# NSA compressed branch and SSD diagonal products issued in another form in a two-layer decoder trunk (one Trainium2 core)

## Chip, cores and metric

The kernel runs on one core of one Trainium2 chip. The metric is the device time of one execution in microseconds (us), lower is better. Before the change it is 2308.91 us, the median of 3 runs (2308.01 to 2309.33).

## The reference

A causal sequence of 256 tokens with 2048 channels goes through two layers, all in float32. Layer 0 mixes with Mamba-2 SSD (16 heads of 64 channels) beside MoBA attention (8 heads of 128); layer 1 mixes with NSA attention (8 query heads, 2 key/value heads of 128) beside retention (8 heads). Each layer ends in a convolutional feed-forward part, and every half layer in a layer norm. What matters here is two sums.

NSA adds three gated attentions for every query head; with 256 tokens the selected blocks and the window both hold all past keys, and the compressed branch has 15 keys per key/value head:

```
k_cmp = compress(kc, ...); v_cmp = compress(vc, ...)     # 15 rows of 128 per kv head
logits_c = q . k_cmp * scale + bias_c;  p_cmp = masked_softmax(logits_c, cmp_mask);  o_cmp = p_cmp . v_cmp
o = g[..., 0:1] * o_cmp + g[..., 1:2] * o_sel + g[..., 2:3] * o_win
```

SSD's part inside its one chunk of 256 tokens is, per head:

```
y_diag = einsum('bgcls,bghcls,bcsghp->bclghp', cb, decay, xdt_g)
```

## The kernel before

Weights stream from HBM in slabs of up to 128 x 1024 values: SP issues the DMA to `wraw` (L102), ScalarE rounds it to the float32r part `whi` (L108), VectorE takes the rest as `wlo` (L109). TensorE multiplies both with activations that lie in SBUF as such pairs. `group_b` (L277) holds weights as the stationary operand; for each 128 rows of the contraction it issues two products of 512 columns with `whi` and two of 256 columns with `wlo` (L314). Here these are called the plain products.

The small work of the mixers is cut into steps and put in a queue, `Fill`. `fill.pop()` after every second contraction step of a group of one output takes the next step out; a step can be empty. So the order of TensorE is: plain products, one step, plain products, one step. The framework then orders the instructions of each engine with a cost model of its own, and each engine works through its queue in order; it puts the semaphore waits in.

`attn_steps` (L599) makes three steps for a head: `scores`, `normalise`, `mix`. It serves MoBA's heads (one branch, no compressed keys) and NSA's (two branches, `ks` and `kw`, with `cmp`). `pair` (L595) queues two heads in turn: two empty steps, scores of both, an empty step, normalise of both, an empty step, mix of both. In `scores` each branch makes the products of 128 queries by 128 keys and 128 by 256 in one PSUM tile `S` (L611, L612); NSA's first branch adds two products with 7 and 15 compressed keys (L615, L616). `softmax` adds bias and finds the row limit on VectorE (L589) and takes exponentials on ScalarE (L592). `normalise` scales by the sum's reciprocal times the gate (L635, for the compressed part L649), turns three tiles of 128 x 128 per branch (L639) and the two compressed ones (L652, L653) and copies them out of PSUM (L642, L644, L655, L656). `mix` (L673) sums, for the first 128 queries and then the other 128, values times turned probabilities: one product per branch in the first half, two in the second, and in each half one with 7 or 15 rows of compressed values `vcmp`. A float32 product is recorded as two loads of the stationary operand and two passes.

`compress` (L1002) makes the compressed keys and values; its step `project` ends with one product for the keys (L1034) and two of 15 columns for the values (L1038), copied into `vcmp`. In `ssd_steps` (L761), `decay` makes the 128 x 384 factor `L` of a head and `diag(ct)` multiplies two heads: three products of 64 columns each (L846 to L848), head 0 into the lower 64 partitions of a PSUM tile and head 1 into the upper 64, all three of head 0 before those of head 1. `odd` (L897) lays out layer 1's buffers; GpSimd only raises to powers there (L199 in the norm ahead of it, L1086 in retention).

Of the kernel before, what the change touches and what calls it, by code (L numbers as in the profile page):

```python
# [9 lines left out]
F32 = mybir.dt.float32  # L10
F32R = mybir.dt.float32r
AF = mybir.ActivationFunctionType
# [248 lines left out]
class Trunk:  # L261
# [321 lines left out]

    def softmax(self, P, S, nb0, nb1, w0, w1, z, stat, j):

        nc = self.nc
        mn = P.tile([128, 2], F32, name="mn", bufs=4)
        for i, (c, n, nb) in enumerate(((0, w0, nb0), (w0, w1, nb1))):
            nc.vector.tensor_tensor_reduce(out=z[:, c:c + n], in0=S[:, c:c + n], in1=nb, scale=SCALE, scalar=3e38,  # L589
                                           op0=OP.add, op1=OP.min, accum_out=mn[:, i:i + 1])  # L590
        for i, (c, n) in enumerate(((0, w0), (w0, w1))):
            nc.scalar.activation(z[:, c:c + n], z[:, c:c + n], AF.Exp, scale=-1.0, bias=mn[:, i:i + 1],  # L592
                                 accum_out=stat[:, j + i:j + i + 1])

# [4 lines left out]
    def attn_steps(self, P, y, ct, h, branches, gate=None, cmp=None):  # L599

        nc = self.nc
        st = {}
        nbr = len(branches)
        ncol = 2 * nbr + (2 if cmp else 0)

        def scores():
            stat = P.tile([128, 8], F32, name="stat", bufs=4)
            st["stat"], st["z"] = stat, []
            for b, (q, k, _) in enumerate(branches):
                S = self.ps()  # L610
                nc.tensor.matmul(S[:, 0:128], q[:, 0:128], k[:, 0:128], start=True, stop=True)  # L611
                nc.tensor.matmul(S[:, 128:384], q[:, 128:256], k, start=True, stop=True)  # L612
                if b == 0 and cmp:
                    kc = cmp[0]
                    nc.tensor.matmul(S[:, 384:391], q[:, 0:128], kc[:, 0:7], start=True, stop=True)  # L615
                    nc.tensor.matmul(S[:, 391:406], q[:, 128:256], kc, start=True, stop=True)  # L616
                z = P.tile([128, 384], F32, name="z", bufs=self.zbufs)
                self.softmax(P, S, self.nb[:, h, 128:256], self.nb[:, h, :], 128, 256, z, stat, 2 * b)
                st["z"].append(z)
                if b == 0 and cmp:  # L620
                    zc = P.tile([128, 22], F32, name="zc", bufs=4)
                    self.softmax(P, S[:, 384:406], self.nb[:, h, 159:256:16], self.nb[:, h, 31:256:16], 7, 15, zc,
                                 stat, 2 * nbr)
                    st["zc"] = zc

        def normalise():
            stat = st["stat"]
            nc.vector.reciprocal(stat[:, :ncol], stat[:, :ncol])
            if gate is not None:
                nc.vector.tensor_tensor(stat[:, :ncol], stat[:, :ncol], gate, op=OP.mult)  # L630
            st["pt"] = []
            for b in range(nbr):
# [12 lines left out]
                st["pt"].append(ptS)  # L645
            if cmp:
                zc = st["zc"]
                for i, (c, n) in enumerate(((0, 7), (7, 15))):
                    nc.vector.tensor_scalar(zc[:, c:c + n], zc[:, c:c + n],  # L649
                                            stat[:, 2 * nbr + i:2 * nbr + i + 1], None, op0=OP.mult)  # L650
# [6 lines left out]
                st["ptc"] = ptc  # L657

        def mix():
            o = self.ps()  # L660
            for t in range(2):
                mms = []
                for b, (_, _, v) in enumerate(branches):
                    pt = st["pt"][b]
                    if t == 0:
                        mms.append((v(0), pt[:, 0:128]))
                    else:
                        mms += [(v(0), pt[:, 128:256]), (v(1), pt[:, 256:384])]
                if cmp:
                    n = 7 if t == 0 else 15  # L670
                    mms.append((cmp[1][:n, :], st["ptc"][:n, t * 128:(t + 1) * 128]))
                for i, (a, b) in enumerate(mms):
                    nc.tensor.matmul(o[:, t * 128:(t + 1) * 128], a, b, start=(i == 0), stop=(i == len(mms) - 1))  # L673
            self.split(y[:, ct, :256], y[:, ct, 256:], o[:, :256])

        return scores, normalise, mix


# [82 lines left out]
    def ssd_steps(self, P, y, dt, xs, bc, zs, mask):  # L761
# [135 lines left out]
    def odd(self):  # L897
        nc, x = self.nc, self.x
        with ExitStack() as ctx:
            self.zbufs = 4  # L900
            with self.tc.tile_pool(name="odd2", bufs=1) as P2:
# [5 lines left out]
                gates = P2.tile([128, H, 6], F32, name="gates")  # L907
                kv = {n: P2.tile([128, 2, 256], F32, name=n) for n in ("ks", "kw")}
                kcmp = P2.tile([128, 30], F32, name="kcmp")
                vcmp = P2.tile([15, 2, 128], F32, name="vcmp")  # L910
                row = P2.tile([128, 1], F32, name="row")
# [45 lines left out]
                for i in range(2):  # L957
                    self.group_b(self.xk, [ev_cmp(i)])
                for i, n in enumerate(("ks", "kw")):
                    self.group_b(self.xk, [lambda acc: self.sum_halves(P2, kv[n], acc)])  # L960
                    self.compress(P2, i, *xbs[i], kcmp, vcmp)
                self.load_bias(P2, P2)
# [3 lines left out]
                for i in range(4):  # L966
# [3 lines left out]
                    for j in range(2):  # L970
# [4 lines left out]
                            P2, y, h, h,  # L975
                            [(q[:, j, :], kv["ks"][:, e, :], lambda t, sl=sl: vs[:, t, sl]),
                             (q[:, j, :], kv["kw"][:, e, :], lambda t, sl=sl: vw[:, t, sl])],
                            gate=gates[:, h, :], cmp=(kcmp[:, 15 * e:15 * e + 15], vcmp[:, e, :])))
                    self.pair(heads)
# [21 lines left out]

    def compress(self, P, i, xh, xl, kcmp, vcmp):  # L1002

# [4 lines left out]
        for s in range(4):  # L1008
# [6 lines left out]
            if s == 3:  # L1015
                rows = P.tile([34, 256], F32, name="crow", bufs=1)
                nc.scalar.activation(rows, acc, AF.Copy)
# [13 lines left out]
        def project():  # L1031
            u, o = st["u"], self.ps()
            if i == 0:
                nc.tensor.matmul(o[:, :30], self.w2[:, 0, :], u, start=True, stop=True)  # L1034
                nc.vector.tensor_copy(kcmp, o[:, :30])
            else:
                for e in range(2):
                    nc.tensor.matmul(o[:15, e * 128:(e + 1) * 128], u[:, 15 * e:15 * e + 15], self.w2[:, 1, :],  # L1038
                                     start=True, stop=True)
                nc.vector.tensor_copy(vcmp.rearrange("p a b -> p (a b)"), o[:15, :256])  # L1040

# [225 lines left out]
```

## Time and profile before

| | before |
|---|---|
| median of 3 runs | 2308.91 us (2308.01 to 2309.33) |
| profiled execution | 2309.18 us, its span 2307.4 us |
| mean granted TensorE clock | 0.998 |
| TensorE busy | 2293.4 us, 99% of the span |
| VectorE, ScalarE, GpSimd busy | 61%, 48%, 1% |
| HBM traffic | 188 GB/s over the span |

The span runs from the first to the last instruction. TensorE's matmuls are pipelined, so the recorded length of one is longer than the time that it holds the engine; the distance between the starts of instructions is what is read. NSA's steps lie between 1304 and 1400 us, SSD's diagonal products between 163 and 221 us.

### The profile page before, as it was taken

The numbers are of one execution on the slowest core, as the hardware profiler recorded it, in microseconds if no ns is written. First come the engines' busy times: TensorE is split into PE (matmuls) and PEld (weight loads), VectorE is DVE, ScalarE is ACT, GpSimd is POOL, SyncE is SP. The second block draws the span as 40 slices with busy tenths as digits, with TensorE's granted clock in tenths as the row PEclk, the third lists the DMA queues.
The fourth block names the chain that finished last, engine by engine and source line by source line (L and its number), as shares of the span: only waits on it lengthen the run. The fifth ranks groups of instructions, "written<-read, shape, count | busy, mean of one in ns | idle before, by whom it ended". The sixth has DMA issues, their size and how long they took to land.

```text
span 2307.4 us, 32010 instructions
## 1 busy us (share of the span) xinstructions
PE 2293.4 (99%) x12550; PEld 1981.4 (86%) x12550; DVE 1418.0 (61%) x1921; ACT 1105.0 (48%) x1429; POOL 21.6 (1%) x32
## 2 busy tenths in 40 slices
PE   9999999999999999999999999999999999999998
PEld 9888888888888888888889888889888888888886
DVE  5687667666666665445645667767666666654445
ACT  5555543555555554334345554444545555543332
POOL 0001000000000000000000000000000000000000
PEclk9999999999999999999999999999999999999999
DMA  8664464666666666667557634584666666676664
GB/s 279 199 188 149 162 226 153 202 191 185 190 189 189 189 197 217 193 193 221 176 166 217 212 108 141 167 269 129 192 189 189 190 190 185 190 226 194 193 194 142
DMA packets 128249, 436.63 MB, mean 189 GB/s; under 512 B 14257, under 2 KB 16993, under 8 KB 127713
## 3 DMA queue, kind: packets, MB, share of 16 engines
q1 hardware_dynamic: 128096, 434.58, 60.9%
q8 instruction: 98, 1.61, 0.3%
q14 instruction: 55, 0.44, 0.1%
HBM read 432.41 MB, written 2.11 MB: 188 GB/s over the span
## 4 chain that ended last, share of the span: by engine, by line
PE 98%; DMA 1%; DVE 1%; ACT 0%; issue 0%; SPq 0%; POOL 0%; DVEq 0%; ACTq 0%; POOLq 0%
PE acc L314 57%; PE acc L353 10%; PE acc L355 10%; PE acc L354 10%; PE ps L353 1%; PE ps L354 1%; PE ps L355 1%; PE ps L673 1%; DMA wraw<-in_ev_in 1%; PE acc L338 1%; PE ps L314 0%; PE ps L252 0%; PE ps L612 0%; PE ps L639 0%; PE ps L338 0%; PE acc L345 0%
## 5 line engine op out<-in xcount | busy, mean ns | idle before, releaser
L109 DVE TENSOR_TENSOR wlo<-wraw,whi 128x1024 fp32r<-128x1024 f32 (+4 forms) x794 | 949.2, 1198 | 635.4 <-ACT whi L108 634.2
L314 PE MATMUL acc<-x,whi 128*128 128x512 f32 x3776 | 1178.3, 397 | 0.0
L108 ACT ACTIVATE whi<-wraw 128x1024 fp32r<-128x1024 f32 (+4 forms) x794 | 822.6, 1037 | 728.6 <-PE acc L355 285.8
L314 PEld LDWEIGHTS acc<-x,wlo 128*128 128x128 f32 x3776 | 692.4, 188 | 156.6 <-issue 0.2
L314 PE MATMUL acc<-x,wlo 128*128 128x256 f32 x3776 | 726.1, 279 | 0.0
L314 PEld LDWEIGHTS acc<-x,whi 128*128 128x128 f32 x3776 | 584.3, 189 | 12.5 <-issue 1.2
L353 PE MATMUL acc<-whi,A 128*128 128x512 f32 x448 | 175.9, 393 | 0.0
L405 ACT ACTIVATE tmp<-acc 128x512 f32<-128x512 f32 x120 | 71.8, 598 | 215.5 <-PE acc L314 215.5
L355 PE MATMUL acc<-whi,A 128*128 128x512 f32 x448 | 174.6, 390 | 0.0
L354 PE MATMUL acc<-wlo,A 128*128 128x512 f32 x448 | 174.5, 390 | 0.0
L353 PE MATMUL acc<-whi,B 128*128 128x512 f32 x388 | 150.9, 389 | 0.0
L354 PE MATMUL acc<-wlo,B 128*128 128x512 f32 x388 | 150.9, 389 | 0.0
L355 PE MATMUL acc<-whi,B 128*128 128x512 f32 x388 | 150.9, 389 | 0.0
L355 PEld LDWEIGHTS acc<-whi,A 128*128 128x128 f32 x448 | 84.1, 188 | 17.7 <-DVE A L274 0.3
L353 PEld LDWEIGHTS acc<-whi,A 128*128 128x128 f32 x448 | 84.1, 188 | 17.3 <-ACT A L273 0.4
L354 PEld LDWEIGHTS acc<-wlo,A 128*128 128x128 f32 x448 | 84.2, 188 | 17.0
L353 PE MATMUL acc<-whi,x 128*128 128x512 f32 (+4 forms) x272 | 93.1, 343 | 0.3 <-ACT V L694 0.3
L354 PE MATMUL acc<-wlo,x 128*128 128x512 f32 (+4 forms) x272 | 92.9, 341 | 0.0
L355 PE MATMUL acc<-whi,x 128*128 128x512 f32 (+4 forms) x272 | 92.8, 341 | 0.0
L353 PEld LDWEIGHTS acc<-whi,B 128*128 128x128 f32 x388 | 72.8, 188 | 15.2
L354 PEld LDWEIGHTS acc<-wlo,B 128*128 128x128 f32 x388 | 72.8, 188 | 15.1
L355 PEld LDWEIGHTS acc<-whi,B 128*128 128x128 f32 x388 | 72.8, 188 | 15.0
(289 smaller groups left out, 1619.7 us busy)
## 6 DMA issues: line engine op xcount, KB each, us to landing
wraw<-in_up SPq DMA_DIRECT2D x328, 512.0 KB, 3.9
wraw<-in_down SPq DMA_DIRECT2D x176, 512.0 KB, 4.3
wraw<-in_od_in SPq DMA_DIRECT2D x96, 512.0 KB, 4.2
wraw<-in_ev_in SPq DMA_DIRECT2D x72, 512.0 KB, 3.5
wraw<-in_ev_out SPq DMA_DIRECT2D x32, 512.0 KB, 4.2
wraw<-in_od_out SPq DMA_DIRECT2D x32, 512.0 KB, 4.5
wraw<-in_up SPq DMA_DIRECT2D x32, 384.0 KB, 3.8
wraw<-in_ev_in SPq DMA_DIRECT2D x16, 348.0 KB, 4.5
```

The source lines that it names most:

```text
L108: nc.scalar.activation(hi[:, :n], raw[:, :n], AF.Copy)
L109: nc.vector.tensor_tensor(lo[:, :n], raw[:, :n], hi[:, :n].bitcast(F32), op=OP.subtract)
L314: nc.tensor.matmul(acc, wt, mv, start=(k == 0 and i < len(unit)), stop=(k == nk - 1 and i >= len(unit)))
L338: nc.tensor.matmul(half(acc, t), slabs[k][0][:, 0, c:c + 128], half(act[k], t), start=(k == 0 and t == 0), stop=False)
L353: nc.tensor.matmul(o, xh, wh, start=first, stop=False)
L354: nc.tensor.matmul(o, xh, wl, start=False, stop=False)
L355: nc.tensor.matmul(o, xl, wh, start=False, stop=last)
L405: nc.scalar.activation(t, a[:, :, 256:], AF.Copy, scale=sign)
L673: nc.tensor.matmul(o[:, t * 128:(t + 1) * 128], a, b, start=(i == 0), stop=(i == len(mms) - 1))
```

## The change

Compressed keys: one tile `kcat` of 272 columns per key/value head holds 16 columns for the compressed keys (15 and a zero) ahead of the 256 selected keys, so that the first branch's two products of `scores` have 144 and 272 columns and the two products of 7 and 15 columns are gone. Compressed probabilities: both heads of a pair write into one tile `zc` of two times 32 columns, zeroed once; the scaling of `zc` stands ahead of that of `z`; only head 1's `normalise` turns it, with two transposes of 32 columns, one in the PSUM tile of each branch, and two copies into 32 rows of a zeroed tile `ptc` of 128 rows. Compressed values: `project` makes four products of 128 columns from a padded operand, so that rows 16j to 16j+14 of `vcmp[:, e, j]` hold the values for head j of a pair and the other rows are zero. `mix`: one product of 256 columns for both halves of the queries and one of 128 for the rest, per branch, and one of 256 columns with 128 rows for the compressed part; this form serves MoBA too. SSD: `diag` issues the three products of both heads in turn. GpSimd zeroes the new tiles at the start of layer 1; `compress` takes its row tile from the buffers `k`. The core of the diff:

```diff
@@ scores
-                nc.tensor.matmul(S[:, 0:128], q[:, 0:128], k[:, 0:128], start=True, stop=True)
-                nc.tensor.matmul(S[:, 128:384], q[:, 128:256], k, start=True, stop=True)
-                if b == 0 and cmp:
-                    kc = cmp[0]
-                    nc.tensor.matmul(S[:, 384:391], q[:, 0:128], kc[:, 0:7], start=True, stop=True)
-                    nc.tensor.matmul(S[:, 391:406], q[:, 128:256], kc, start=True, stop=True)
+                n = k.shape[1] - 256
+                nc.tensor.matmul(S[:, 0:n + 128], q[:, 0:128], k[:, 0:n + 128], start=True, stop=True)
+                nc.tensor.matmul(S[:, n + 128:2 * n + 384], q[:, 128:256], k, start=True, stop=True)
@@ normalise
+            if cmp:
+                zc = cmp[1]
+                for t in range(2):
+                    a = zc[:, t, 16 * j:16 * j + 16]
+                    nc.vector.tensor_scalar(a, a, stat[:, 2 * nbr + t:2 * nbr + t + 1], None, op0=OP.mult)
...
+                if cmp and j:
+                    nc.tensor.transpose(pt[:32, 384:512], cmp[1][:, b, :], self.ident)
...
-                pt = self.ps()
-                nc.tensor.transpose(pt[:7, 0:128], zc[:, 0:7], self.ident)
-                nc.tensor.transpose(pt[:15, 128:256], zc[:, 7:22], self.ident)
-                ptc = P.tile([15, 256], F32, name="ptc", bufs=2)
-                nc.scalar.activation(ptc[:7, 0:128], pt[:7, 0:128], AF.Copy)
-                nc.scalar.activation(ptc[:, 128:256], pt[:15, 128:256], AF.Copy)
+                if cmp and j:
+                    nc.scalar.activation(cmp[2][:32, 128 * b:128 * b + 128], pt[:32, 384:512], AF.Copy)
@@ mix
-            for t in range(2):
...
+            for (_, _, v), pt in zip(branches, st["pt"]):
+                mms += [(o[:, 0:256], v(0), pt[:, 0:256]), (o[:, 128:256], v(1), pt[:, 256:384])]
+            if cmp:
+                mms.append((o[:, 0:256], cmp[0][:, j, :], cmp[2]))
@@ ssd_steps, diag
-                for j in range(2):
-                    h = 2 * ct + j
-                    L, o = st.pop(h), ps[64 * j:64 * j + 64, :]
-                    xh = [xdt[:, t, 64 * h:64 * h + 64] for t in range(2)]
-                    nc.tensor.matmul(o[:, 0:128], xh[0], L[:, 0:128], start=True, stop=True)
-                    nc.tensor.matmul(o[:, 128:256], xh[0], L[:, 128:256], start=True, stop=False)
-                    nc.tensor.matmul(o[:, 128:256], xh[1], L[:, 256:384], start=False, stop=True)
+                Ls = [st.pop(2 * ct + j) for j in range(2)]
+                for l, t, c, first, last in ((0, 0, 0, True, True), (128, 0, 128, True, False), (128, 1, 256, False, True)):
+                    for j in range(2):
+                        h = 2 * ct + j
+                        nc.tensor.matmul(ps[64 * j:64 * j + 64, l:l + 128], xdt[:, t, 64 * h:64 * h + 64],
+                                         Ls[j][:, c:c + 128], start=first, stop=last)
@@ odd
+                kcat = P2.tile([128, 2, 272], F32, name="ks")
+                zcs = [P2.tile([128, 2, 32], F32, name=f"zc{i}") for i in range(2)]
+                ptcs = [P2.tile([128, 256], F32, name=f"ptc{i}") for i in range(2)]
+                for t in (kcat[:, :, 0:16], *zcs, *ptcs):
+                    nc.gpsimd.memset(t, 0.0)
@@ compress, project of the values
+                pad = P.tile([128, 2, 256], F32, name="k", bufs=2).rearrange("p e (j c) -> p e j c", j=2)
+                nc.vector.memset(pad, 0.0)
+                for j in range(2):
+                    nc.vector.tensor_copy(pad[:, :, j, 16 * j:16 * j + 15], u.rearrange("p (e m) -> p e m", e=2))
                 for e in range(2):
-                    nc.tensor.matmul(o[:15, e * 128:(e + 1) * 128], u[:, 15 * e:15 * e + 15], self.w2[:, 1, :],
-                                     start=True, stop=True)
+                    for j in range(2):
+                        c = 256 * e + 128 * j
+                        nc.tensor.matmul(o[:, c:c + 128], pad[:, e, j, :], self.w2[:, 1, :], start=True, stop=True)
```

## Rows read from the trace of the kernel before

**Rows 1.** The page: busy time of each engine, and the chain that ended last, by engine.

```profile
PE 2293.4 (99%) x12550; PEld 1981.4 (86%) x12550; DVE 1418.0 (61%) x1921; ACT 1105.0 (48%) x1429; POOL 21.6 (1%) x32
...
PE 98%; DMA 1%; DVE 1%; ACT 0%; issue 0%; SPq 0%; POOL 0%; DVEq 0%; ACTq 0%; POOLq 0%
```

**Rows 2.** Busy time by stage: the stretch in us, its length, then busy us and instructions of PE, PEld, DVE, ACT and POOL, the granted clock, DMA share and GB/s. SSD's stretch, the feed-forward part of layer 0, NSA's stretch.

```profile
125.00:235.00 110.00, 110.00 (x690) 95.39 (x689) 86.66 (x163) 55.71 (x82) 7.79 (x8) 1.00 0.53 169
...
420.00:1080.00 660.00, 660.00 (x3513) 566.93 (x3512) 386.02 (x419) 320.17 (x367) 0.00 (x0) 1.00 0.63 193
...
1304.00:1400.00 96.00, 96.00 (x601) 83.94 (x600) 61.97 (x211) 52.32 (x154) 0.00 (x0) 1.00 0.36 112
```

**Rows 3.** Timeline of TensorE around the scores of NSA's head 0: start in us, us, engine, line, operation, tiles, shapes, count. The later groups of rows from a timeline have the same columns.

```profile
1304.47 0.63 PE L314 MATMUL acc<-x,whi 128*128 128x512 f32 x2
1304.93 0.40 PE L314 MATMUL acc<-x,wlo 128*128 128x256 f32 x2
1305.16 0.38 PE L611 MATMUL ps<-ks,q 128*128 128x128 f32 x2
...
1305.82 0.28 PE L615 MATMUL ps<-kcmp,q 128*128 128x7 f32 x2
1305.96 0.37 PE L616 MATMUL ps<-kcmp,q 128*128 128x15 f32 x2
1306.18 0.47 PE L611 MATMUL ps<-kw,q 128*128 128x128 f32 x2
...
1307.38 0.40 PE L314 MATMUL acc<-x,wlo 128*128 128x256 f32 x2
```

**Rows 4.** Timeline of TensorE around the scores of a MoBA head (one branch); left out between the two rows are L611 x2, L612 x2 and two plain products of 512 columns.

```profile
238.12 0.39 PE L314 MATMUL acc<-x,wlo 128*128 128x256 f32 x2
...
239.47 0.40 PE L314 MATMUL acc<-x,wlo 128*128 128x256 f32 x2
```

**Rows 5.** Timeline of TensorE around the transposes of NSA's head 0; left out are L652 x1 and two plain products of 512 columns.

```profile
1312.61 0.40 PE L314 MATMUL acc<-x,wlo 128*128 128x256 f32 x2
1312.85 0.82 PE L639 MATMUL ps<-ident,z 128*128 128x128 f32 x6
...
1313.61 0.27 PE L653 MATMUL ps<-ident,zc 128*15 128x128 f32 x1
...
1314.18 0.40 PE L314 MATMUL acc<-x,wlo 128*128 128x256 f32 x2
```

**Rows 6.** Timeline of TensorE around the mix of NSA's head 0.

```profile
1318.57 0.40 PE L314 MATMUL acc<-x,wlo 128*128 128x256 f32 x2
...
1319.02 0.39 PE L673 MATMUL ps<-pt,vw 128*128 128x128 f32 x2
1319.34 0.48 PE L673 MATMUL ps<-ptc,vcmp 7*128 7x128 f32 x2
1319.75 0.71 PE L673 MATMUL ps<-pt,vs 128*128 128x128 f32 x4
...
1320.84 0.48 PE L673 MATMUL ps<-ptc,vcmp 15*128 15x128 f32 x2
...
1321.83 0.39 PE L314 MATMUL acc<-x,wlo 128*128 128x256 f32 x2
```

**Rows 7.** Timeline of TensorE around the mix of a MoBA head; left out are L673 x6 and two plain products of 512 columns.

```profile
249.89 0.39 PE L314 MATMUL acc<-x,wlo 128*128 128x256 f32 x2
...
251.25 0.40 PE L314 MATMUL acc<-x,wlo 128*128 128x256 f32 x2
```

**Rows 8.** Timeline of TensorE around the products of the compressed values; two plain products of 512 columns are left out.

```profile
1300.02 0.39 PE L314 MATMUL acc<-x,wlo 128*128 128x256 f32 x2
1300.34 0.61 PE L1038 MATMUL ps<-prm,cu 128*15 128x128 f32 x4
...
1301.45 0.39 PE L314 MATMUL acc<-x,wlo 128*128 128x256 f32 x2
```

**Rows 9.** Timeline of TensorE at the first pair of SSD heads: head 0's first product, head 1's first product, head 0's fourth pass, and the plain product behind both.

```profile
163.45 0.43 PE L846 MATMUL ps<-L,xdt 128*64 128x128 f32 x2
...
163.72 0.32 PE L846 MATMUL ps<-L,xdt 128*64 128x128 f32 x1
163.83 0.27 PE L847 MATMUL ps<-L,xdt 128*64 128x128 f32 x1
...
164.52 0.73 PE L314 MATMUL acc<-x,whi 128*128 128x512 f32 x2
```

**Rows 10.** Timeline of TensorE at the last pair of SSD heads, with plain products between the two heads.

```profile
218.47 0.43 PE L846 MATMUL ps<-L,xdt 128*64 128x128 f32 x2
...
219.82 0.43 PE L846 MATMUL ps<-L,xdt 128*64 128x128 f32 x2
...
220.62 0.96 PE L314 MATMUL acc<-x,whi 128*128 128x512 f32 x3
```

**Rows 11.** Timeline of VectorE ahead of the transposes of NSA's head 0.

```profile
1311.36 1.01 DVE L635 TENSOR_SCALAR z<-z,stat 128x128 f32<-128x128 f32 x4
1312.29 0.36 DVE L649 TENSOR_SCALAR zc<-zc,stat 128x7 f32<-128x7 f32 x2
```

**Rows 12.** Timeline of ScalarE ahead of the mix of NSA's head 0: the last copy of head 1's compressed probabilities, and the next instruction.

```profile
1317.77 0.25 ACT L656 ACTIVATE ptc<-ps 15x128 f32<-15x128 f32 x1
1318.81 1.06 ACT L108 ACTIVATE whi<-wraw 128x1024 fp32r<-128x1024 f32 x1 [0.79 <-ACT ptc L656]
```

More of the change, by code (lines that the diff above doesn't have):

```diff
@@ L582, in load_bias, with softmax @@
             nc.vector.tensor_copy(self.nb[:, 2 * a:2 * a + 2, :], t[:, :, ::-1])
-    def softmax(self, P, S, nb0, nb1, w0, w1, z, stat, j):
+    def softmax(self, P, parts, stat, j):
         nc = self.nc
         mn = P.tile([128, 2], F32, name="mn", bufs=4)
-        for i, (c, n, nb) in enumerate(((0, w0, nb0), (w0, w1, nb1))):
-            nc.vector.tensor_tensor_reduce(out=z[:, c:c + n], in0=S[:, c:c + n], in1=nb, scale=SCALE, scalar=3e38,
+        for i, (S, nb, z) in enumerate(parts):
+            nc.vector.tensor_tensor_reduce(out=z, in0=S, in1=nb, scale=SCALE, scalar=3e38,
                                            op0=OP.add, op1=OP.min, accum_out=mn[:, i:i + 1])
-        for i, (c, n) in enumerate(((0, w0), (w0, w1))):
-            nc.scalar.activation(z[:, c:c + n], z[:, c:c + n], AF.Exp, scale=-1.0, bias=mn[:, i:i + 1],
-                                 accum_out=stat[:, j + i:j + i + 1])
+        for i, (S, nb, z) in enumerate(parts):
+            nc.scalar.activation(z, z, AF.Exp, scale=-1.0, bias=mn[:, i:i + 1], accum_out=stat[:, j + i:j + i + 1])
     def pair(self, heads, waits=(2, 1, 1)):
@@ L604, in attn_steps @@
         ncol = 2 * nbr + (2 if cmp else 0)
+        j = h % 2
         def scores():
@@ L610, in scores @@
                 S = self.ps()
-                nc.tensor.matmul(S[:, 0:128], q[:, 0:128], k[:, 0:128], start=True, stop=True)
-                nc.tensor.matmul(S[:, 128:384], q[:, 128:256], k, start=True, stop=True)
-                if b == 0 and cmp:
-                    kc = cmp[0]
-                    nc.tensor.matmul(S[:, 384:391], q[:, 0:128], kc[:, 0:7], start=True, stop=True)
-                    nc.tensor.matmul(S[:, 391:406], q[:, 128:256], kc, start=True, stop=True)
+                n = k.shape[1] - 256
+                nc.tensor.matmul(S[:, 0:n + 128], q[:, 0:128], k[:, 0:n + 128], start=True, stop=True)
+                nc.tensor.matmul(S[:, n + 128:2 * n + 384], q[:, 128:256], k, start=True, stop=True)
                 z = P.tile([128, 384], F32, name="z", bufs=self.zbufs)
-                self.softmax(P, S, self.nb[:, h, 128:256], self.nb[:, h, :], 128, 256, z, stat, 2 * b)
+                self.softmax(P, [(S[:, n:n + 128], self.nb[:, h, 128:256], z[:, 0:128]),
+                                 (S[:, 2 * n + 128:2 * n + 384], self.nb[:, h, :], z[:, 128:384])], stat, 2 * b)
                 st["z"].append(z)
-                if b == 0 and cmp:
-                    zc = P.tile([128, 22], F32, name="zc", bufs=4)
-                    self.softmax(P, S[:, 384:406], self.nb[:, h, 159:256:16], self.nb[:, h, 31:256:16], 7, 15, zc,
+                if n:
+                    zc = cmp[1]
+                    self.softmax(P, [(S[:, 0:7], self.nb[:, h, 159:256:16], zc[:, 0, 16 * j:16 * j + 7]),
+                                     (S[:, n + 128:n + 143], self.nb[:, h, 31:256:16], zc[:, 1, 16 * j:16 * j + 15])],
                                  stat, 2 * nbr)
-                    st["zc"] = zc
         def normalise():
@@ L645, in normalise @@
                 st["pt"].append(ptS)
[L646 to L650, printed above, removed]
-                pt = self.ps()
-                nc.tensor.transpose(pt[:7, 0:128], zc[:, 0:7], self.ident)
-                nc.tensor.transpose(pt[:15, 128:256], zc[:, 7:22], self.ident)
-                ptc = P.tile([15, 256], F32, name="ptc", bufs=2)
-                nc.scalar.activation(ptc[:7, 0:128], pt[:7, 0:128], AF.Copy)
-                nc.scalar.activation(ptc[:, 128:256], pt[:15, 128:256], AF.Copy)
-                st["ptc"] = ptc
+                if cmp and j:
+                    nc.scalar.activation(cmp[2][:32, 128 * b:128 * b + 128], pt[:32, 384:512], AF.Copy)
         def mix():
             o = self.ps()
-            for t in range(2):
[L662 to L673, printed above, removed]
+            mms = []
+            for (_, _, v), pt in zip(branches, st["pt"]):
+                mms += [(o[:, 0:256], v(0), pt[:, 0:256]), (o[:, 128:256], v(1), pt[:, 256:384])]
+            if cmp:
+                mms.append((o[:, 0:256], cmp[0][:, j, :], cmp[2]))
+            for i, (d, a, b) in enumerate(mms):
+                nc.tensor.matmul(d, a, b, start=(i == 0), stop=(i == len(mms) - 1))
             self.split(y[:, ct, :256], y[:, ct, 256:], o[:, :256])
@@ L907, in odd @@
                 gates = P2.tile([128, H, 6], F32, name="gates")
-                kv = {n: P2.tile([128, 2, 256], F32, name=n) for n in ("ks", "kw")}
-                kcmp = P2.tile([128, 30], F32, name="kcmp")
-                vcmp = P2.tile([15, 2, 128], F32, name="vcmp")
+                kcat = P2.tile([128, 2, 272], F32, name="ks")
+                kw = P2.tile([128, 2, 256], F32, name="kw")
+                vcmp = P2.tile([128, 2, 2, 128], F32, name="vcmp")
+                zcs = [P2.tile([128, 2, 32], F32, name=f"zc{i}") for i in range(2)]
+                ptcs = [P2.tile([128, 256], F32, name=f"ptc{i}") for i in range(2)]
+                for t in (kcat[:, :, 0:16], *zcs, *ptcs):
+                    nc.gpsimd.memset(t, 0.0)
                 row = P2.tile([128, 1], F32, name="row")
@@ L958, in odd @@
                     self.group_b(self.xk, [ev_cmp(i)])
-                for i, n in enumerate(("ks", "kw")):
-                    self.group_b(self.xk, [lambda acc: self.sum_halves(P2, kv[n], acc)])
-                    self.compress(P2, i, *xbs[i], kcmp, vcmp)
+                for i, d in enumerate((kcat[:, :, 16:272], kw)):
+                    self.group_b(self.xk, [lambda acc: self.sum_halves(P2, d, acc)])
+                    self.compress(P2, i, *xbs[i], kcat, vcmp)
                 self.load_bias(P2, P2)
@@ L975, in odd @@
                             P2, y, h, h,
-                            [(q[:, j, :], kv["ks"][:, e, :], lambda t, sl=sl: vs[:, t, sl]),
-                             (q[:, j, :], kv["kw"][:, e, :], lambda t, sl=sl: vw[:, t, sl])],
-                            gate=gates[:, h, :], cmp=(kcmp[:, 15 * e:15 * e + 15], vcmp[:, e, :])))
+                            [(q[:, j, :], kcat[:, e, :], lambda t, sl=sl: vs[:, t, sl]),
+                             (q[:, j, :], kw[:, e, :], lambda t, sl=sl: vw[:, t, sl])],
+                            gate=gates[:, h, :], cmp=(vcmp[:, e], zcs[i % 2], ptcs[i % 2])))
                     self.pair(heads)
@@ L1000, in odd, with compress @@
         self.out_rest(yk, 2)
-    def compress(self, P, i, xh, xl, kcmp, vcmp):
+    def compress(self, P, i, xh, xl, kcat, vcmp):
         nc, w = self.nc, self.w
@@ L1015, in compress @@
             if s == 3:
-                rows = P.tile([34, 256], F32, name="crow", bufs=1)
+                rows = P.tile([128, 2, 256], F32, name="k", bufs=2)[:34, 0, :]
                 nc.scalar.activation(rows, acc, AF.Copy)
```

5 lines of the change are left out of this document (3 added, 2 removed).

## Prediction

> **What bounds the kernel now.** I read the page first: TensorE is busy 99% of the span, and the chain that ended last is TensorE for 98% [rows 1]. The reader is to see that no other engine has a share of that chain worth naming, so that time that TensorE doesn't need any more is time off the end, as long as its operands arrive. Then the stages: in SSD's stretch and in NSA's TensorE has no idle time at all and its clock is granted in full, while VectorE has 87 of 110 us and 62 of 96, ScalarE 56 and 52 [rows 2]. So each part is priced in TensorE's time. A recorded matmul is longer than its place in the stream; I take distances between starts. Two plain passes of 512 columns take 1304.93 - 1304.47 = 0.46 us and two of 256 take 0.23 [rows 3], so the four plain products that lie in every window below are 0.69, and what is left of a window belongs to the step in it.
>
> **Scores.** From the plain product ahead to the one behind, head 0 of NSA takes 1307.38 - 1304.93 = 2.45, less 0.69 = 1.76 us [rows 3]. A MoBA head, with one branch and no compressed keys, takes 239.47 - 238.12 - 0.69 = 0.66 for two passes of 128 and two of 256 columns, 768 in all, or 0.86 ns per column [rows 4]. Two branches are 1.32, so the four short passes of 7 and 15 columns cost 0.44: 0.11 each, as much as a pass of 128 columns. The wider products add 4 times 16 columns, 64 x 0.86 ns = 0.055. Gain 0.385 a head, 3.1 for eight.
>
> **Transposes.** Six of `z` and two of the compressed probabilities take 1314.18 - 1312.61 - 0.69 = 0.88, so 0.11 each; the two small ones show no gap ahead or behind [rows 5]. A pair has four small ones now and two after: 0.22 x 4 pairs = 0.9. The new ones have 32 columns where these have 7 and 15; I take the same price.
>
> **Mix.** NSA's step is 1321.83 - 1318.57 - 0.69 = 2.57 us [rows 6]. MoBA's six passes of 128 columns take 251.25 - 249.89 - 0.69 = 0.67 [rows 7], so NSA's twelve full ones are 1.34 and the compressed ones, two visits with two passes each, 1.23. The rows show where that goes: the pass pair ahead of the first visit starts at 1319.02 and needs 0.22, yet the visit starts at 1319.34, and the next full product 0.41 after that; the engine empties at both edges of a visit with 7 or 15 rows. After the change each branch streams 2 x 256 + 2 x 128 = 768 columns, as now, so 0.67, and the compressed product, with all 128 rows and no such edge, 512 columns at 0.86 ns = 0.44. The step becomes 1.78. Gain 0.79 a head, 6.3 for eight. MoBA's mix streams the same columns with two loads less; I count nothing (0.67 against the 0.66 of rows 4 leaves 0.1 us for eight heads at most).
>
> **Compressed values.** Four passes of 15 columns take 1301.45 - 1300.02 - 0.69 = 0.74 with their edges [rows 8]; eight of 128 columns at 0.11 take 0.88. Cost 0.1. The zeroing and two copies ahead of it on VectorE are covered by the plain products until 1304.
>
> **SSD.** A head alone, from its first product to the plain one behind, takes 220.62 - 219.82 = 0.80 [rows 10]; a pair takes 164.52 - 163.45 = 1.07, because head 1 starts 0.27 after head 0 [rows 9]. From then on both run beside each other, in the two halves of the columns: head 1's first product starts ahead of head 0's fourth pass [rows 9]. In the new order two of head 0's passes stand ahead of head 1's first, not six. No row shows that order. The gain lies between 0 (the halves hinder each other) and 0.27 (they start together); a lag in proportion to what is queued ahead, 2/6 of 0.27, leaves a gain of 0.18, nearest to the rows; I take 0.2, for seven pairs 1.4. The last pair runs as two visits, 0.80 each, at 218.47 and 219.82 [rows 10]; together they would take 0.89. Gain 0.7, between 0 (the planner still sends head 0's first product ahead alone) and 0.8.
>
> **Waits that are added.** (a) The scaling of `zc`, 0.36 us for two [rows 11], now stands ahead of that of `z` on VectorE, which ends at 1312.37 where the transposes begin at 1312.85 [rows 5, 11]: cover 0.48. Scores that are 0.385 shorter bring the transposes nearer by up to as much, so what is left is between +0.48 - 0.36 and 0.48 - 0.36 - 0.385, a wait of 0 to 0.27 a head, 0 to 2.2 in all, with the plain products queued behind it. TensorE's order is planned so that some plain products fill such gaps; I take 0.5. (b) Head 0's mix needs the copies that follow head 1's transposes; that is a rival below. (c) The product with the selected keys now needs the compressed keys too; their step is queued ahead of the first scores. (d) GpSimd's zeroing at the start of layer 1 has no work behind it until retention's powers; it is 1% busy [rows 1]. No DMA is moved.
>
> **Sum.** 3.1 + 0.9 + 6.3 - 0.1 + 1.4 + 0.7 - 0.5 = 11.8 us. Against the profiled execution, 2309.18 (span 2307.4 and 1.8 around it), that is 2297.4; the profiled one is 0.27 above the median of the runs, so 2297.1.
>
> **A rule that speaks against a term.** The four short passes of the scores take 0.11 us each in the trace [rows 3]. The Trainium skill, "TensorE: Matmul & The Clock Gate", section "Back-to-back issue gap", lets a matmul of 1 to 64 columns pass in some 60 cycles, about 25 ns. By that the four cost 0.1, the first term is 8 x (0.1 - 0.055) = 0.4 in place of 3.1, and the sum an estimated 9.1. The row decides: each short pass waits for a stationary operand of 128 columns like a full one, and that load goes away with it.
>
> **Rivals.**
> - *The 0.44 of the short passes isn't freed*, because it is the full product behind them that waits, whatever stands ahead. Then only the 0.055 is added, the scores lose 0.4 in place of gaining 3.1, and the time is 2300.6. For it: the pass behind the short ones starts late. Against: a MoBA head, without them, shows 0.66 and no such remainder [rows 4]. The page above is the rule beside it. Chance 0.05.
> - *The weights can't follow.* A step that is shorter asks for the next slab sooner; TensorE would then wait for `whi` and `wlo`. Half the gain lost gives 2303.0. Against: with NSA's stretch at 86 us, VectorE would be at 62/86 = 72% and ScalarE at 61%, and in the feed-forward part plain products without pause are fed at 386/660 = 58% and no idle time [rows 2]. Chance 0.06.
> - *SSD's second head blocks the queue.* Head 1's product is now second in TensorE's order; if its `L` is late, all plain products behind wait. The price is the distance of the two heads, 1.35 us [rows 10]; on eight pairs 10.8, and SSD's 2.1 are gone: 11.8 - 2.1 - 10.8 = -1.1, so 2310.0, no change. Against: seven of eight pairs run as one visit now, so both `L` are there. Chance 0.04.
> - *Slower: head 0's mix waits for head 1's copies.* They end at 1318.02 [rows 12]; head 0's compressed product, last in the new mix, would start about 1318.80 + 1.34 = 1320.1. So 2.1 us of cover. It costs more than the rest gains from 2.1 + 11.8/4 = 5.0 us of delay on each of four pairs; 6 us late give 15.6 - 11.8 = 3.8, and 7.0 are beyond 0.2%: 4 x 4.9 - 11.8 = +7.8, 2316.7. Against: what stands ahead of a copy on ScalarE is a rounding of 1.06 [rows 12]. Chance 0.03.
>
> **How the numbers follow.** The forecast has the remaining 0.82. Its own ends: SSD at 0.27 and 0.8, no wait, MoBA's 0.1 give 13.0; with some 0.03 of rounding on each of the 24 NSA steps and the order planned anew, 14.4, so 2294.5. SSD at nothing and the wait at 2.2 give 8.0, so 2300.9. The first rival lies inside; the range is 2294.5 to 2301.0. About 0.2%, 4.6 us, is what a measurement of this kernel can tell from no change, so faster means below 2304.3: forecast, first and nearly all of the second rival, 0.91. Within 0.2%: 0.06. Slower: 0.03.
>
> **What would show it.** The windows measured above, in the trace after: scores 1.37 (from 1.76), head 1's transposes with two more and head 0's with none, mix 1.78 (from 2.57) without a gap in it, SSD pairs under 0.9 (from 1.07) with head 1's first product within 0.1 of head 0's; NSA's stretch some 9.5 us shorter with TensorE still without idle time. Wrong would be: idle time of TensorE ahead of L639's or L673's successors, an edge at the 32-column transposes, or SSD's halves taking turns.

## The result, and the profile after

The changed kernel takes 2296.22 us, the median of 4 runs (2295.51 to 2297.65), against 2308.91 before: 12.7 us less, ratio 0.9947 with a 95% interval of 0.9934 to 0.9959. Its profiled execution took 2296.87 with a span of 2295.1, 12.3 below the span before. The forecast was 2297.1, the range 2294.5 to 2301.0.

What bounds it hasn't changed: the page's busy line and its chain by engine, which answer to [rows 1].

```profile
PE 2280.7 (99%) x12450; PEld 1970.8 (86%) x12450; DVE 1419.1 (62%) x1924; ACT 1104.2 (48%) x1421; POOL 22.0 (1%) x37
...
PE 98%; DVE 1%; DMA 1%; ACT 0%; issue 0%; POOL 0%; DVEq 0%; POOLq 0%
```

TensorE's busy time fell by 12.7 us and the other engines' hardly moved. The window over NSA's stretch (the columns of [rows 2]), now 86.4 us long where it was 96, shows that TensorE has 0.15 us of idle time in it, VectorE at 61.79/86.40 = 72%:

```profile
1300.50:1386.90 86.40, 86.25 (x517) 76.18 (x516) 61.79 (x211) 51.78 (x146) 0.00 (x0) 1.00 0.43 128
```

Scores of NSA's head 0, timeline of TensorE, against [rows 3]. The short products are gone; from plain product to plain product it is 1304.82 - 1302.76 = 2.06 us, less 0.69 for the plain ones 1.37 (1.76 before).

```profile
1302.76 0.39 PE L314 MATMUL acc<-x,wlo 128*128 128x256 f32 x2
1302.99 0.41 PE L612 MATMUL ps<-ks,q 128*128 128x144 f32 x2
1303.24 0.62 PE L613 MATMUL ps<-ks,q 128*128 128x272 f32 x2
...
1304.82 0.40 PE L314 MATMUL acc<-x,wlo 128*128 128x256 f32 x2
```

Transposes of NSA's head 0, which has no small ones any more, and then two of the instructions of head 1, which turns the compressed probabilities of both (timeline of TensorE, against [rows 5]): head 0 takes 1311.02 - 1309.66 - 0.69 = 0.67 us (0.88 before), and the small transpose (L644) is followed after 0.11 by the next full one, so it has no edge.

```profile
1309.66 0.40 PE L314 MATMUL acc<-x,wlo 128*128 128x256 f32 x2
...
1311.02 0.40 PE L314 MATMUL acc<-x,wlo 128*128 128x256 f32 x2
...
1314.14 0.27 PE L644 MATMUL ps<-ident,zc 128*32 128x128 f32 x1
1314.25 0.49 PE L642 MATMUL ps<-ident,z 128*128 128x128 f32 x3
```

Mix of the third NSA head, timeline of TensorE, against [rows 6]: 1339.72 - 1337.29 - 0.69 = 1.74 us (2.57 before). The compressed product follows the full ones in step: 0.66 after the start of the four ahead, as these stand 0.65 apart.

```profile
1337.29 0.40 PE L314 MATMUL acc<-x,wlo 128*128 128x256 f32 x2
1337.52 0.82 PE L662 MATMUL ps<-pt,vs 128*128 128x256 f32 x4
1338.17 0.82 PE L662 MATMUL ps<-pt,vw 128*128 128x256 f32 x4
1338.83 0.60 PE L662 MATMUL ps<-ptc,vcmp 128*128 128x256 f32 x2
...
1339.72 0.40 PE L314 MATMUL acc<-x,wlo 128*128 128x256 f32 x2
```

The first pair of SSD heads, timeline of TensorE, against [rows 9]: all twelve passes in one row, and 164.48 - 163.67 = 0.81 us to the plain product behind (1.07 before), as long as one head alone takes in [rows 10].

```profile
163.67 0.88 PE L835 MATMUL ps<-L,xdt 128*64 128x128 f32 x12
164.48 0.73 PE L314 MATMUL acc<-x,whi 128*128 128x512 f32 x2
```

The last pair, which answers to [rows 10], is still two visits: head 14's first product alone, and 1.4 us later the other ten passes.

```profile
216.73 0.43 PE L835 MATMUL ps<-L,xdt 128*64 128x128 f32 x2
217.09 0.39 PE L314 MATMUL acc<-x,wlo 128*128 128x256 f32 x1
...
218.10 0.87 PE L835 MATMUL ps<-L,xdt 128*64 128x128 f32 x10
218.90 0.50 PE L314 MATMUL acc<-x,whi 128*128 128x512 f32 x1
```

Where TensorE waits on the new steps, there are two places. The first is the last pair's transposes: timeline of TensorE, then of VectorE. Between the first of its eight transposes and the plain product behind the last lie 1378.91 - 1377.25 = 1.66 us, for eight transposes (0.88) and two plain passes (0.46): 0.3 too many. The transposes at 1378.14 wait for the scaling of `z` (L638), which stands behind the weights' part `wlo` (L109) and a copy. The scaling of `zc` (L634), which the change put ahead, took 0.37 us of that queue; whether that is what costs is tried below.

```profile
1377.25 0.27 PE L642 MATMUL ps<-ident,z 128*128 128x128 f32 x1
1377.28 0.71 PE L314 MATMUL acc<-x,whi 128*128 128x512 f32 x2
1378.14 0.44 PE L642 MATMUL ps<-ident,z 128*128 128x128 f32 x2 [0.15 <-DVE z L638]
...
1378.91 0.48 PE L314 MATMUL acc<-x,wlo 128*128 128x256 f32 x2
```

```profile
1375.67 0.37 DVE L634 TENSOR_SCALAR zc<-zc,stat 128x16 f32<-128x16 f32 x2
...
1376.14 1.22 DVE L109 TENSOR_TENSOR wlo<-wraw,whi 128x1024 fp32r<-128x1024 f32 x1
1377.28 0.55 DVE L649 COPY pt<-ps 128x384 f32<-128x384 f32 x1
1377.75 0.80 DVE L638 TENSOR_SCALAR z<-z,stat 128x256 f32<-128x256 f32 x3
```

The second is the first pair's mix: timeline of TensorE, then of ScalarE. The compressed product starts 0.72 after the four ahead of it, where the third head's starts 0.66 after, and its second pass is late as well: the step takes 1317.96 - 1315.39 - 0.69 = 1.88 us, 0.14 more than the 1.74 above. The second copy of the compressed probabilities (L652) starts at 1316.60, behind a rounding of 1.06, and ends at 1316.60 + 0.25 = 1316.85, just ahead of the product at 1316.99.

```profile
1315.39 0.40 PE L314 MATMUL acc<-x,wlo 128*128 128x256 f32 x2
...
1316.27 0.82 PE L662 MATMUL ps<-pt,vw 128*128 128x256 f32 x4
1316.99 0.67 PE L662 MATMUL ps<-ptc,vcmp 128*128 128x256 f32 x2
...
1317.96 0.40 PE L314 MATMUL acc<-x,wlo 128*128 128x256 f32 x2
```

```profile
1315.63 1.06 ACT L108 ACTIVATE whi<-wraw 128x1024 fp32r<-128x1024 f32 x1 [0.55 <-ACT ptc L652]
1316.60 0.25 ACT L652 ACTIVATE ptc<-ps 32x128 f32<-32x128 f32 x1
```

### The profile page after: what moved, and what is told of

Read it like the earlier page. It is cut to its first block, busy times and chain, and to the rows that moved or that the text cites. A ratio compares the mean times of both kernels' runs of the same rounds, so it can differ in the third digit from the quotient of the medians.

```text
span 2295.1 us, 31817 instructions
## 1 busy us (share of the span) xinstructions
PE 2280.7 (99%) x12450; PEld 1970.8 (86%) x12450; DVE 1419.1 (62%) x1924; ACT 1104.2 (48%) x1421; POOL 22.0 (1%) x37
## 4 chain that ended last, share of the span: by engine, by line
PE 98%; DVE 1%; DMA 1%; ACT 0%; issue 0%; POOL 0%; DVEq 0%; POOLq 0%
PE acc L314 57%; PE acc L353 10%; PE acc L355 10%; PE acc L354 10%; PE ps L355 1%; PE ps L353 1%; PE ps L354 1%; PE ps L662 1%; PE acc L338 1%; PE ps L314 0%; PE ps L252 0%; PE ps L613 0%; DMA wraw<-in_ev_in 0%; PE acc L345 0%; PE ps L338 0%; PE ps L642 0%
## 5 line engine op out<-in xcount | busy, mean ns | idle before, releaser
L109 DVE TENSOR_TENSOR wlo<-wraw,whi 128x1024 fp32r<-128x1024 f32 (+4 forms) x794 | 949.5, 1197 | 630.9 <-ACT whi L108 629.3
```

The source lines that it names most:

```text
L109: nc.vector.tensor_tensor(lo[:, :n], raw[:, :n], hi[:, :n].bitcast(F32), op=OP.subtract)
```

## Experiments

My theory was that each part is worth its own time on TensorE: columns, edges between products of 128 and of fewer rows, a load of the stationary operand per short pass, and the lag between two heads. The rivals were that the parts hang together or are given back in a later wait, that the number of products is what counts, and that short passes cost their columns. Each run stands beside the kernel before on the same chip: 2308.92 us beside the first four, 2308.44 beside the next four, 2309.43 beside the last three. That kernel itself differs by 1.0 us from chip to chip, so a difference of some tenths between runs of different chips is read from traces, not from totals.

### SSD alone, and the attention alone

The first is the kernel before with the new `diag`; the second the changed kernel with the old one:

```diff
-                for l, t, c, first, last in ((0, 0, 0, True, True), (128, 0, 128, True, False), (128, 1, 256, False, True)):
-                    for j in range(2):
...
+                for j in range(2):
...
+                    nc.tensor.matmul(o[:, 0:128], xh[0], L[:, 0:128], start=True, stop=True)
+                    nc.tensor.matmul(o[:, 128:256], xh[0], L[:, 128:256], start=True, stop=False)
+                    nc.tensor.matmul(o[:, 128:256], xh[1], L[:, 256:384], start=False, stop=True)
```

The diff is that of the second; the first is the diff of `diag` quoted with the change, and nothing else.

> The kernel before with only the SSD products of two heads issued in turn. Theory (each part is worth its own time on TensorE and the parts add): the seven pairs lose 0.27 us each, the last pair up to 0.5, so 2.1 to 2.4 us less than before, about 2306.6; pair 0.81 us from its first product to the plain one behind. Rival (the parts need each other, or the time goes to a later wait): no change of the total although the pairs are shorter.

> The changed kernel with SSD's products in the old order, head by head. Theory (the parts add): 2.1 to 2.4 us more than the changed kernel, about 2298.5, which is 10.3 less than before; together with the run that has SSD alone the sum is the whole change, 12.3 to 12.7. Rival: the sum of the two parts is off by more than 1 us.

Measured: SSD alone 2306.55, 2.4 less than before, ratio 0.9989 (0.9979 to 0.9998); its pair takes 0.81. Attention alone 2298.23, 10.7 less, ratio 0.9950 (0.9934 to 0.9967). The two sum to 13.1, the whole change is 12.7; the difference is within the runs' spread. The parts add, and nothing is given back later. The timeline of TensorE at the first pair, SSD alone:

```profile
165.24 0.88 PE L846 MATMUL ps<-L,xdt 128*64 128x128 f32 x12
166.05 0.73 PE L314 MATMUL acc<-x,whi 128*128 128x512 f32 x2
```

### The compressed product with 32 rows

```diff
-                mms.append((o[:, 0:256], cmp[0][:, j, :], cmp[2]))
+                mms.append((o[:, 0:256], cmp[0][:32, j, :], cmp[2][:32, :]))
```

> The changed kernel, but the compressed product of the mix takes the 32 rows that hold probabilities instead of all 128 (the other 96 are zero). Theory (the old product lost its time where the engine empties between products of 128 rows and of fewer): the edges come back, about 0.4 us for each of eight heads, so 3 us more than the changed kernel, about 2299.3, and the mix takes 2.2 after the four plain products are taken off, from 1.78. Rival (what counts is the number of products and of loads): no change, 2296.2.

Measured: 2299.31, 3.1 us above the changed kernel. The mix of head 0 takes 1317.94 - 1315.11 - 0.69 = 2.14 us against 1.74 for a mix that doesn't wait (the third head's), 0.4 more, with the same two passes of 256 columns. In the timeline of TensorE the 32-row visit starts 0.75 after the four passes ahead, not 0.65 or 0.66, and the plain products begin 0.62 after it.

```profile
1315.11 0.40 PE L314 MATMUL acc<-x,wlo 128*128 128x256 f32 x2
...
1316.00 0.82 PE L662 MATMUL ps<-pt,vw 128*128 128x256 f32 x4
1316.75 0.69 PE L662 MATMUL ps<-ptc,vcmp 32*128 32x256 f32 x2
1317.37 0.73 PE L314 MATMUL acc<-x,whi 128*128 128x512 f32 x2
1317.94 0.40 PE L314 MATMUL acc<-x,wlo 128*128 128x256 f32 x2
```

So 128 rows, of which 113 are zeros in the values of one head, are cheaper than 32. The rival (number of products) falls.

### The mix in halves

```diff
+            for t in range(2):
...
+                    mms.append((v(0), pt[:, 128 * t:128 * t + 128]))
+                    if t:
+                        mms.append((v(1), pt[:, 256:384]))
+                if cmp:
+                    mms.append((cmp[0][:, j, :], cmp[2][:, 128 * t:128 * t + 128]))
...
+                    nc.tensor.matmul(o[:, t * 128:(t + 1) * 128], a, b, start=(i == 0), stop=(i == len(mms) - 1))
```

> The changed kernel, but every product of the mix is made for 128 queries at a time (with all 128 rows): more passes and loads, the same columns. Theory (the mix costs columns and edges, and a load of 128 columns hides behind a pass of 128): no change, within 0.5 us of the changed kernel, the mix at 1.78. Rival (fewer products are what saves): the eight NSA heads lose 8 passes to 16; at the 0.03 us or more that a pass would cost beside its columns, 2 us more for 16 heads.

Measured: 2296.71, 0.5 above the changed kernel, at the rim of what runs can tell. The mix takes 1317.57 - 1315.09 - 0.69 = 1.79 against 1.74: 0.05 for six passes more, 0.008 each. That is a quarter of what the rival needed. So the wider products have some 0.4 us of the 12.7 in NSA's eight heads. The window in the timeline of TensorE:

```profile
1315.09 0.40 PE L314 MATMUL acc<-x,wlo 128*128 128x256 f32 x2
...
1317.57 0.40 PE L314 MATMUL acc<-x,wlo 128*128 128x256 f32 x2
```

### Short products of 64 columns

```diff
-                    nc.tensor.matmul(S[:, 384:391], q[:, 0:128], kc[:, 0:7], start=True, stop=True)
-                    nc.tensor.matmul(S[:, 391:406], q[:, 128:256], kc, start=True, stop=True)
+                    nc.tensor.matmul(S[:, 384:448], q[:, 0:128], kc, start=True, stop=True)
+                    nc.tensor.matmul(S[:, 448:512], q[:, 128:256], kc, start=True, stop=True)
```

Here `kc` has 64 columns, of which 49 are zero; the rest of the edit makes that tile, zeroes it once on GpSimd and tells `softmax` where the scores lie.

> The kernel before, but the short products of the scores have 64 columns each (7 or 15 compressed keys, the rest zero) in place of 7 and 15. Theory (a short pass is held up by the load of its 128 stationary columns, 0.11 us): no change of the scores' window, 2.45 us at head 0, and of the total, 2308.9. Rival (a short pass costs its columns beside a fixed part): 2 x (57 + 49) columns more a head at 0.86 ns, 0.18 us a head and 1.5 us in all, 2310.4.

Measured: 2308.62 against 2308.44 before, ratio 0.9999 (0.9990 to 1.0009). Head 0's window is 1306.33 - 1303.86 = 2.47, from 2.45 for 22 columns to 2.47 for 128: up to 64 columns a pass costs 0.02 us a head more, so the columns are as good as free. In the trace of the kernel before, the loads of the stationary operand of these passes start (1306.15 - 1305.93) / 2 = 0.11 apart, which is the price of a pass; so the pass costs what its load costs. A short pass with a smaller stationary operand, which would part the load from any other fixed cost, was not tried. Timeline of TensorE, then two rows of the loads (PEld) in the kernel before:

```profile
1303.86 0.40 PE L314 MATMUL acc<-x,wlo 128*128 128x256 f32 x2
...
1306.33 0.40 PE L314 MATMUL acc<-x,wlo 128*128 128x256 f32 x2
```

```profile
1305.93 0.30 PEld L616 LDWEIGHTS ps<-kcmp,q 128*128 128x128 f32 x2
1306.15 0.30 PEld L611 LDWEIGHTS ps<-kw,q 128*128 128x128 f32 x2
```

### The last SSD pair one step later

```diff
-        steps += [diag(7), 4, rms(1), 1, scale(1)]
+        steps += [1, diag(7), 3, rms(1), 1, scale(1)]
```

> The changed kernel with one empty step ahead of the last pair of SSD heads and one fewer behind it. Theory (the planner sent head 14's first product ahead because head 15's factor was not ready, and each visit to a half of the columns costs its two edges): the last pair goes as one visit like the others, 0.6 us less, about 2295.6. Rival (the split comes from elsewhere): two visits still, no change.

Measured: 2295.08, 1.1 below the changed kernel's median (the ranges overlap, 2294.75 to 2296.84; by the kernel before on the same chip it is 13.4 less where the change had 12.7), and in the trace one visit of twelve passes, 218.22 - 217.41 = 0.81 us, in place of two of 0.36 and 0.80 with their edges. The trace settles it, the total only agrees: the visits are 0.36 + 0.80 - 0.81 = 0.35 us shorter, and an edge is gone. In the changed kernel head 15's factor was late: VectorE makes it (L824) from 216.69 to 217.24, and head 14's first product starts at 216.73. Timeline of TensorE:

```profile
217.41 0.88 PE L835 MATMUL ps<-L,xdt 128*64 128x128 f32 x12
218.22 0.73 PE L314 MATMUL acc<-x,whi 128*128 128x512 f32 x2
```

### The scaling of the compressed probabilities behind that of z

```diff
-            if cmp:
+            def scale_zc():
                 zc = cmp[1]
...
             for b in range(nbr):
...
+                if cmp and b == 1 - j:
+                    scale_zc()
```

> The changed kernel with the scaling of the compressed probabilities behind that of z: behind both branches for head 0, behind the first for head 1. Theory (the scaling ahead of z is what makes the transposes of the second heads late, split by plain products, with TensorE idle 0.2 us once): the idle time ahead of the transposes goes, 0.3 to 1 us less, about 2295.6. Rival (it is the weights' part wlo on VectorE, 1.22 us each, that stands ahead of z): no change.

Measured: 2295.98, 0.2 below the changed kernel: inconclusive by time. In the trace the idle time of TensorE ahead of the transposes of `z` (here L645) is gone from the list of waits, but the last pair's transposes are still cut up by plain products, and that costs the same: with eight transposes and two plain passes in it, the stretch takes 1380.07 - 1378.43 = 1.64 us against 1.66. The weights' part still stands between the scalings of `z` on VectorE. So the theory falls, the scaling's place isn't what costs the 0.3 us, and the rival (the weights' part is what stands ahead) holds as far as one run goes. Timeline of TensorE:

```profile
1378.43 0.49 PE L645 MATMUL ps<-ident,z 128*128 128x128 f32 x3
...
1380.07 0.48 PE L314 MATMUL acc<-x,wlo 128*128 128x256 f32 x2
```

### No empty step ahead of the mix

```diff
-                    self.pair(heads)
+                    self.pair(heads, (2, 1, 0))
```

> The changed kernel without the empty step between normalise and mix of a pair, so that the first mix comes some 1.4 us sooner. Theory (the copies of the compressed probabilities have little cover left: 0.1 us of waiting was there once in four pairs): TensorE waits ahead of the compressed product, or takes plain products ahead of it, 0 to 1.3 us in each of four pairs, 1 to 4 us more in all. Rival (there is cover of about 2 us): no change.

Measured: 2297.25, 1.0 above the changed kernel, with ranges that overlap (by the kernel before on the same chip 1.5 above); at the low end of what was expected. The trace shows both answers that were named. In the first pair the planner puts a plain pass ahead of the compressed product; in the last TensorE waits: from the second four passes the compressed product starts 1379.55 - 1378.81 = 0.74 later, and 0.54 pass from there to the next head's first, where 0.44 is its length. The chain behind that is the copy: on ScalarE it waits for VectorE's copy of the same PSUM tile. First TensorE, then ScalarE:

```profile
1378.81 0.82 PE L662 MATMUL ps<-pt,vw 128*128 128x256 f32 x4
1379.55 0.70 PE L662 MATMUL ps<-ptc,vcmp 128*128 128x256 f32 x2
1380.09 0.82 PE L662 MATMUL ps<-pt,vs 128*128 128x256 f32 x4
```

```profile
1379.23 0.27 ACT L652 ACTIVATE ptc<-ps 32x128 f32<-32x128 f32 x1 [0.68 <-DVE pt L649]
```

So the rival of the late copies is a real mechanism with a price of 0.09 + 0.10 = 0.2 us in the last pair; the cover of 2.1 us that I had counted was not there, and still TensorE lost little. That the planner also moved other plain products is part of this run, so its total isn't the price of the wait alone.

### Four passes of head 0 ahead of head 1

```diff
-                for l, t, c, first, last in (...):
-                    for j in range(2):
+                for j, i in ((0, 0), (0, 1), (1, 0), (1, 1), (0, 2), (1, 2)):
```

> The changed kernel with SSD's products of a pair in the order head 0, head 0, head 1, head 1, head 0, head 1: four passes of head 0 ahead of head 1's first, between six (before, lag 0.27 us) and two (the change). What sets the lag of head 1? Theory (a share of what is queued ahead, as the prediction had it): 4/6 of 0.27 = 0.18, the pair 0.98 us, 1.2 us more in seven pairs. Rival (head 1 goes as soon as the passes ahead of it fit in what is held for head 0's half; three passes had begun when it went before): a lag of 0.06 or less, the pair 0.81 to 0.87, 0.4 us more at most.

Measured: 2296.04, no change, and the pair takes 163.29 - 162.48 = 0.81. My theory falls: the lag is not in proportion to what is queued ahead. With two passes ahead and with four the halves start together; with six head 1 was 0.27 late. The trace's single starts lie 0.007 us apart with two and 0.013 with four, a step more for each product ahead, so the queue follows the order of the text here. With six a late factor isn't the reason: in the kernel before, VectorE ends the factors of the first pair (L835) at 160.75 + 0.55 = 161.30, head 1 starts at 163.72, and the pair takes 1.07 us in each of the seven. Why six are too many was not tried. Timeline of TensorE at the first pair:

```profile
162.48 0.88 PE L836 MATMUL ps<-L,xdt 128*64 128x128 f32 x12
163.29 0.50 PE L314 MATMUL acc<-x,whi 128*128 128x512 f32 x1
```

### Both mends together

The edits of the last SSD pair and of the scaling, in one kernel, beside the changed kernel run again.

> The changed kernel with both mends: an empty step ahead of the last SSD pair, and the scaling of the compressed probabilities behind that of z. Theory (the two measured savings add): 0.6 to 1.2 us less than the changed kernel run beside it, about 2295.2. Rival (VectorE's order is planned anew and gives some of it back): no difference from the changed kernel.

> The changed kernel once more, as a measure for the run beside it. 2296.2 within 0.5 by every theory.

Measured: 2295.41 (2294.54 to 2297.69) beside 2296.45 (2296.20 to 2297.18), 1.0 less by the medians, with ranges that overlap. The run with the SSD step alone had 2295.08 on another chip, too near to tell from this; the traces showed a gain from the SSD step and none from the scaling's place. The later step of the last SSD pair is the one worth keeping.

## Why the prediction was right

**Bound.** TensorE was the bound and stayed it; each microsecond taken from it came off the end.

**Scores.** 1.37 us after, as forecast; the gain is 0.39 a head, 3.1 in all. The price of a short pass was right and for the right reason: 64 columns cost what 7 and 15 did. The first rival is out. The 25 ns for a matmul of 1 to 64 columns, which the prediction took from the Trainium skill ("TensorE: Matmul & The Clock Gate", section "Back-to-back issue gap") as a rule against this term, is there the gap of a matmul by itself; for a stream of loads and matmuls the same section says that both set the distance. The trace agrees: each short pass brings its own load of 128 columns, and [rows 3] and the run with 64 columns show 0.11 us. So that page spoke for the term.

**Transposes.** The first head of each pair loses its two, 0.21 us a pair, and the new ones with 32 columns show no edge: 0.84 for the 0.9 forecast.

**Mix.** 1.74 us against 1.78 forecast; 0.83 a head, 6.5 in all after the 0.14 of waiting. The run with 32 rows gives back 3.1 us of it, which is the edges of one visit; what remains, 2.57 - 2.14 = 0.43 a head, is that one visit with two passes took the place of two with four. MoBA's mix takes 249.04 - 247.69 - 0.69 = 0.66 against 0.67 [rows 7], so it was right to count nothing there.

**Compressed values.** 1299.26 - 1297.67 - 0.69 = 0.90 after (from plain product to plain product, as in [rows 8]) against 0.74: a cost of 0.16, where the prediction's working had 0.14 and its sum 0.1.

**SSD.** Here a term was mis-sized. The seven pairs gained 0.26 each, 1.8 for the 1.4 forecast: "a lag in proportion to what is queued ahead" was the wrong way to fill the gap between the bounds, and the end of the bound (they start together) was right. The last pair gained 0.44 in place of 0.7, because the planner sent head 14's first product ahead, one of the two ends that the prediction had named. The two errors nearly cancel, 1.8 + 0.44 = 2.2 against 2.1, and that is luck.

**Waits.** This term was mis-sized too, and its cause isn't the one that was named. 0.5 was forecast for the scaling of `zc`. The trace has about 0.3 at the transposes of one of eight heads, but with the scaling behind that of `z` they take the same (1.64 against 1.66), so no run shows a price of the scaling; what stands ahead in both is the weights' part and a copy. That 0.3 lies near 0.5 is luck. And there is 0.14 at one mix, which the prediction held to be covered by 2.1 us. That cover took for granted that both copies follow the transposes at once, as before. The second one now shares a PSUM tile with a copy on VectorE and can't pass it (the run without the empty step shows that wait, 0.68), and in the first pair it was queued behind one rounding more, so that of the cover nothing was left.

Summed from the windows: 3.1 + 0.84 - 0.3 + 6.5 - 0.16 + 1.8 + 0.44 = 12.2, and the spans differ by 12.3. These are windows of one head or pair times their number. The rivals of the weights and of the slower end show nothing in the trace, except for the 0.14; where SSD's second head was late, in the last pair, the planner put plain products between and nothing was blocked.

## What to carry to other kernels

When one engine is busy 99% of the span, price an edit by distances between the starts of neighbouring instructions, with the known stream around it taken off; such windows gave the steps of scores, transposes, mix and compressed values here to within a tenth of a microsecond each; the terms without a row of their own (SSD's new order, the waits) were the ones that came out otherwise. Look first for small products that cost an edge or a load of their own: append their columns to a product that is there anyway, and pad a short contraction with zeros so that it joins the stream of full ones. A step that takes on work for its neighbour needs its cover counted anew, with every engine that touches the same PSUM tile in the queue.

## What the hardware showed that was not expected

- Two products into the two halves of the columns start together (0.81 us for a pair, one head alone 0.80) when two or four passes of the first stand ahead of the second in the queue, and 0.27 us apart with six.
- A float32 product of 32 rows (two passes of 256 columns) among products of 128 costs 0.4 us more (2.14 against 1.74 for the mix) than the same with 128 rows, of which 96 are zeros in both operands.
- Cutting products of 256 columns into two of 128 costs 0.008 us a pass (1.79 against 1.74 for six passes more), so the loads of 128 stationary columns hide almost wholly behind passes of 128.
